# Another order of the first eight seven-product steps at each feed-forward start

## The chip, the cores and the metric

One core of a Trainium2 chip runs the whole program. The metric is the device time of one execution in microseconds (us); lower is better. Three runs of the kernel before gave 3456.26, 3458.66 and 3461.72 us, so its median is 3458.66 us.

## The reference

Two small networks run one after the other on one sequence of 512 rows of width 1024. The first has two layers of feed-forward, mixer, feed-forward; the second has two layers of mixer, feed-forward. Six feed-forward blocks in all, each

```python
def swiglu(h, w1, w3, w2):
    return (jax.nn.silu(h @ w1) * (h @ w3)) @ w2
```

with `w1` and `w3` of 1024 x 2816 and `w2` of 2816 x 1024, in float32 (in the second network these are the gate, up and down matrices). In the first network a layer's shifts, scales and gates are vectors that come from `silu(c) @ ada_w[l] + ada_b[l]`. The mixers (attention, spatial gating and a state-space scan; a gated delta rule and a short convolution) and the norms between the blocks are not touched by the change.

## The kernel before

A float32 product is made on TensorE (PE) from two rounded parts of each operand, a high and a low one: `mm3` (L102 to L107) issues high x high (L105), high x low (L106) and low x high (L107). A weight block is split by `split` (L87 to L93): ScalarE (ACT) casts it into `whi` (L90), VectorE (DVE) subtracts and writes `wlo` (L91). The hidden 2816 columns are 22 tiles of 128, the f-tiles. `ffn` (L502) does the first two of them as plain products of 512 columns (the bank `p`), then `pair_products` (L411 to L495) does the other 20 as ten pairs, i = 1 to 10. For a pair it splits the 1024-deep product into 2 x 2 blocks and makes seven block products of the kind of Strassen and Winograd in place of eight, for `w1` (w = 0) and `w3` (w = 1). One of the seven, called (i, m) here with m from 0 to 6, is 24 matmuls of 128 x 256: 2 weights x 4 chunks x 3.

- The right operands, `rhs[m]`, are quarters of the input or sums of quarters. `half_sums` (L363 to L388) makes these at each start on DVE (`bq`, and the splits into `ta` and `t`).
- The left operands come from `left` (L390 to L409). For m = 0, 1 and 4 they are raw blocks of the weights as loaded; for m = 5, 2, 3 and 6 DVE first makes a sum `sw` (L397), and (i, 2) needs the sum of (i, 5), (i, 6) that of (i, 2).
- `prepare(k + 3)` (L428 to L440) makes the split of a product three places ahead of its use in the list `seq`; the pool for `whi` and `wlo` has three buffers. `load` (L420) brings raw halves of 512 KB with SyncE's (SP's) queue (L264). The pool of raw halves has four buffers, and `nrx` more: one in the four feed-forward blocks of the first network, two in those of the second (L1758, L1863).
- In PSUM, (i, 0) opens a bank `a` and (i, 5) a bank `h`. When (i, 0) is done, ACT copies `a` to one of two banks `chain` (L478), the one of number i mod 2, and the products 2, 3 and 4 are added on there. When (i, 2) is done, ACT copies `chain` to SBUF as `sq` (L481), when (i, 3) is done once more (L487); the next product into that bank has to wait for such a copy. (i, 1) is added on to `a`, which ACT and DVE then read (L456, L457); (i, 6) is added on to `h`.
- While the first network's feed-forward blocks run, `tick` (called once per product) lets `ada_all` (L165 on) do a step of the ada vectors: a load of 512 KB (`adaraw`, L159) and one DVE instruction (L173, L175).

The order in which the products are asked for is the list `seq` (L424 to L426). A scheduler then puts the instructions on each engine in an order that it picks by its own costs, and each engine runs its own in that order. So the order on PE, ACT, DVE and SP follows from `seq`, from the buffers and from that scheduler; it is fixed when the program is built.

The starts of the six feed-forward blocks, counted from the first matmul of (1, 0), are at 65.40, 744.51, 1108.34, 1782.84, 2465.68 and 3128.11 us of the profiled execution; they are called start 1 to start 6 below.

Of the kernel before, what the change touches and what calls it, by code (L numbers as in the profile page):

```python
# [48 lines left out]
class Net:  # L49
# [361 lines left out]
    def pair_products(self, w1, w3, rhs, pool, g32, tick):  # L411


        nc = self.nc
        n = NF // 2
        raws, sts, slots = {}, {}, {}
        loads = [(i, w, k) for i in range(1, n) for k in range(2) for w in range(2)]
        ring = itertools.count()

        def load(upto):  # L420
            while loads and loads[0][0] <= upto:
                i, w, k = loads.pop(0)
                raws[i, w, k] = self.raw_half((w1, w3)[w], i * 256, k, pool if next(ring) % (4 + self.nrx) >= 4 else None)
        seq = [(1, 0)]  # L424
        for i in range(1, n):
            seq += [(i, 5), (i, 2), (i, 1), (i, 3)] + [(i + 1, 0)] * (i + 1 < n) + [(i, 4), (i, 6)]  # L426

        def prepare(k):  # L428
            if k >= len(seq):
                return  # L430
            i, m = seq[k]
            load(i)
            hi = self.wsp.tile([128, 2, 4, 128], F32R, tag="hi", name="whi")
            lo = self.wsp.tile([128, 2, 4, 128], F32R, tag="lo", name="wlo")
            for w in range(2):
                x = self.left([raws[i, w, 0], raws[i, w, 1]] if m else [raws[i, w, 0]], m, sts.setdefault((i, w), {}), pool)
                self.split(hi[:, w], lo[:, w], x)
            slots[k] = hi, lo
            if m == 5:
                load(i + 1)  # L440
        L, R = slice(0, 256), slice(256, 512)
        chain = [self.abank("chain") for _ in range(2)]
        for c in chain:

            nc.tensor.matmul(c, self.onesr, rhs[2][0].rearrange("p k n -> p (k n)")[:, 0:512], start=True, stop=True)
        for k in range(3):
            prepare(k)
            yield
        a, h, u, gs = {}, {}, {}, {}
        gtile = lambda: pool.tile([128, T], F32, tag="g", name="g", bufs=NF)  # L450
        utile = lambda: pool.tile([128, 512], F32, tag="sq", name="sq", bufs=4)

        def gated(o, x):

            s = pool.tile([128, 256], F32, tag="si", name="si", bufs=2)
            nc.scalar.activation(s, x[:, L], AF.Silu)  # L456
            nc.vector.tensor_tensor(o, s, x[:, R], op=ALU.mult)  # L457

        def gated_add(o, x, y):

            nc.vector.tensor_tensor(y, x, y, op=ALU.add)
            nc.scalar.activation(y[:, L], y[:, L], AF.Silu)  # L462
            nc.gpsimd.tensor_tensor(o, y[:, L], y[:, R], op=ALU.mult)  # L463
        for k, (i, m) in enumerate(seq):
            if m == 0:
                a[i] = self.gbank("a")
            if m == 5:
                h[i] = self.gbank("h")
            b = chain[i % 2]
            bank = {0: a, 1: a, 5: h, 6: h}.get(m, {i: b})[i]  # L470
            hi, lo = slots.pop(k)
            for w in range(2):
                for kc in range(4):
                    first = m in (0, 5) and w == 0 and kc == 0
                    self.mm3(bank[:, 256 * w:256 * w + 256], hi[:, w, kc], lo[:, w, kc], rhs[m][0][:, kc], rhs[m][1][:, kc], first, w == 1 and kc == 3,
                             skip=m not in (0, 5))
            if m == 0:
                nc.scalar.copy(b, bank)  # L478
            elif m == 2:
                u[i, 2] = utile()  # L480
                nc.scalar.copy(u[i, 2], b)  # L481
            elif m == 1:
                gs[i] = [gtile(), gtile()]
                gated(gs[i][0][:, L], a.pop(i))
            elif m == 3:
                u[i, 3] = utile()
                nc.scalar.copy(u[i, 3], b)  # L487
                gated_add(gs[i][1][:, R], h[i], u.pop((i, 3)))
            elif m == 4:
                gated(gs[i][1][:, L], b)  # L490
            elif m == 6:
                gated_add(gs[i][0][:, R], h.pop(i), u.pop((i, 2)))
                g32 += gs.pop(i)
            prepare(k + 3)
            tick(0)  # L495
# [1424 lines left out]
```

## Time and profile before

| | |
|---|---|
| median of three runs | 3458.66 us (3456.26 to 3461.72) |
| the profiled execution | 3459.09 us, its span 3457.4 us |
| PE busy | 3341.9 us, 97% of the span |
| DVE, ACT, POOL busy | 73%, 46%, 11% |
| granted TensorE clock, mean over the span | 0.989 |

PE is TensorE's matmuls, PEld its weight loads. A row of the timeline gives the start, the length, the engine, the line and the operation of an instruction, then in brackets how long its engine was idle before it and what ended that. Matmuls are pipelined: a row of 0.28 us is followed by the next after about 0.12 us where nothing is waited for. A row of a view by stretches gives the busy time of each engine between two times, the granted clock as a share of full speed, and what the DMA engines did.

### The profile page before, as it was taken

To read this page: it belongs to the slowest core of one execution; us is meant where nothing else is said; L and a number is where in the kernel's file an instruction comes from. 1 tells how busy PE (TensorE), PEld (TensorE's weight loads), DVE (VectorE), ACT (ScalarE), POOL (GpSimd) and SP (SyncE) were. 2 spreads that over 40 slices of the span, in tenths; PEclk is the share of its full clock that TensorE was granted. 3 is DMA by queue.
4 is the path that set the end of the run, shared out by engine and by line. 5 is a ranking of instruction groups with operands and counts; after the bars stand their busy time and mean duration, and the time that the engine had idled before them with its cause. 6 is when DMAs were issued, how large, how long until landed. Compare 5 with 4: busy or idle time off the path is not lost.

```text
span 3457.4 us, 56915 instructions
## 1 busy us (share of the span) xinstructions
PE 3341.9 (97%) x22138; PEld 2893.9 (84%) x22138; DVE 2530.1 (73%) x4666; ACT 1597.5 (46%) x3331; POOL 372.1 (11%) x427
## 2 busy tenths in 40 slices
PE   7999999999999999989999998999999999999999
PEld 6998776689988998866689987778999877789987
DVE  7997677789877997777789846765786357559753
ACT  3553336545533553336645533534555345345542
POOL 0221000002200210000001101101121001011200
PEclk9999999999999999999999999999999999999999
DMA  7558251335563557251334442213333321233332
GB/s 248 177 172 268 85 153 50 99 104 159 161 211 109 165 162 253 86 154 50 98 104 135 128 135 82 62 51 121 110 98 123 120 70 45 62 130 108 123 108 75
DMA packets 316270, 428.51 MB, mean 124 GB/s; under 512 B 24222, under 2 KB 255168, under 8 KB 316000
## 3 DMA queue, kind: packets, MB, share of 16 engines
q1 hardware_dynamic: 309884, 423.22, 38.3%
q8 instruction: 174, 2.85, 0.3%
q10 hardware_dynamic: 6116, 1.65, 0.2%
q14 instruction: 96, 0.79, 0.1%
HBM read 401.22 MB, written 23.59 MB: 123 GB/s over the span
## 4 chain that ended last, share of the span: by engine, by line
PE 83%; DVE 8%; ACT 3%; DMA 2%; issue 2%; POOL 1%; SPq 0%; DVEq 0%; POOLq 0%; ACTq 0%
PE acc L106 8%; PE acc L107 8%; PE acc L105 8%; PE chain L105 5%; PE chain L107 5%; PE chain L106 5%; PE g L105 4%; PE g L106 3%; PE g L107 3%; PE h L107 3%; PE h L105 3%; PE h L106 3%; PE a L107 3%; PE a L105 3%; PE a L106 3%
## 5 line engine op out<-in xcount | busy, mean ns | idle before, releaser
L91 DVE TENSOR_TENSOR wlo<-raw,whi 128x512 fp32r<-128x512 f32 (+1 forms) x700 | 534.6, 784 | 344.2 <-ACT whi L90 336.5
L90 ACT CAST whi<-raw 128x512 fp32r<-128x512 f32 (+1 forms) x700 | 473.9, 696 | 627.7 <-PE acc L107 234.4
L106 PE MATMUL acc<-wlo,ghi 128*128 128x512 f32 x992 | 393.1, 396 | 0.0
L90 ACT CAST whi<-sw 128x512 fp32r<-128x512 f32 x480 | 291.2, 618 | 219.2 <-PE chain L106 100.4
L107 PE MATMUL acc<-whi,glo 128*128 128x512 f32 x992 | 391.5, 395 | 0.0
L105 PE MATMUL acc<-whi,ghi 128*128 128x512 f32 x992 | 391.1, 394 | 0.0
L463 POOL TENSOR_TENSOR g<-sq 128x256 f32<-128x256 f32 x120 | 242.7, 2022 | 1163.1 <-ACT sq L462 1073.3
L91 DVE TENSOR_TENSOR wlo<-sw,whi 128x512 fp32r<-128x512 f32 x480 | 322.8, 689 | 46.8 <-ACT whi L90 46.6
L107 PE MATMUL a<-hThi,wlo 128*128 128x256 f32 x960 | 270.3, 282 | 11.6 <-DVE wlo L91 11.6
L105 PE MATMUL chain<-t,whi 128*128 128x256 f32 x960 | 269.8, 281 | 8.1 <-ACT sq L487 8.1
L105 PE MATMUL g<-hThi,whi 128*128 128x512 f32 x576 | 239.5, 416 | 32.0 <-DVE oT L895 23.2
L105 PE MATMUL a<-hThi,whi 128*128 128x256 f32 x960 | 269.9, 281 | 0.0
L106 PE MATMUL a<-hTlo,whi 128*128 128x256 f32 x960 | 269.4, 281 | 0.0
L107 PE MATMUL chain<-t,wlo 128*128 128x256 f32 x960 | 269.1, 280 | 0.0
L106 PE MATMUL chain<-t,whi 128*128 128x256 f32 x960 | 269.0, 280 | 0.0
L106 PE MATMUL g<-hTlo,whi 128*128 128x512 f32 x576 | 236.2, 410 | 0.0
L107 PE MATMUL g<-hThi,wlo 128*128 128x512 f32 x576 | 235.5, 409 | 0.0
L105 PEld LDWEIGHTS acc<-whi,ghi 128*128 128x128 f32 x992 | 186.3, 188 | 46.1 <-issue 0.3
L106 PEld LDWEIGHTS acc<-wlo,ghi 128*128 128x128 f32 x992 | 186.3, 188 | 44.3
L107 PEld LDWEIGHTS acc<-whi,glo 128*128 128x128 f32 x992 | 186.2, 188 | 43.7
L397 DVE TENSOR_TENSOR sw<-raw 128x512 f32<-128x512 f32 x240 | 165.1, 705 | 52.2 <-DMA raw<-in_ffn_w_gate_dram 23.3
L107 PEld LDWEIGHTS a<-hThi,wlo 128*128 128x128 f32 x960 | 181.2, 189 | 13.0 <-DVE wlo L91 13.0
(480 smaller groups left out, 8756.9 us busy)
## 6 DMA issues: line engine op xcount, KB each, us to landing
raw<-in_ffn_w_dram SPq DMA_DIRECT2D x264, 512.0 KB, 4.3
adaraw<-in_ada_w_dram SPq DMA_DIRECT2D x128, 512.0 KB, 4.7
raw<-in_w_in_dram SPq DMA_DIRECT2D x136, 256.0 KB, 3.6
raw<-in_ffn_w_gate_dram SPq DMA_DIRECT2D x44, 512.0 KB, 4.0
raw<-in_ffn_w_up_dram SPq DMA_DIRECT2D x44, 512.0 KB, 4.9
raw<-in_ffn_w_down_dram SPq DMA_DIRECT2D x44, 512.0 KB, 3.3
xdram<-x SPq DMA_DIRECT2D x36, 512.0 KB, 2.6
x<-xdram SPq DMA_DIRECT2D x36, 512.0 KB, 7.0
```

What stands on the lines that cost most here:

```text
L90: self.last_copy = self.nc.scalar.copy(hi, src)
L91: self.last_rest = (eng or self.nc.vector).tensor_tensor(lo, src, hi.bitcast(F32), op=ALU.subtract)
L105: mm(out, w_hi, m_hi, start=start, stop=False, skip_group_check=skip)
L106: mm(out, w_hi, m_lo, start=False, stop=False, skip_group_check=skip)
L107: mm(out, w_lo, m_hi, start=False, stop=stop, skip_group_check=skip)
L397: nc.vector.tensor_tensor(o, x, y, op=op)
L463: nc.gpsimd.tensor_tensor(o, y[:, L], y[:, R], op=ALU.mult)
```

## The change

The list `seq` gets other first entries; from the pair i = 2 on it is as it was.

```diff
-        seq = [(1, 0)]
-        for i in range(1, n):
+
+        seq = [(1, 0), (1, 1), (2, 0), (1, 5), (1, 2), (1, 3), (1, 4), (1, 6)]
+        for i in range(2, n):
             seq += [(i, 5), (i, 2), (i, 1), (i, 3)] + [(i + 1, 0)] * (i + 1 < n) + [(i, 4), (i, 6)]
```

Before, the list began (1, 0), (1, 5), (1, 2), (1, 1), (1, 3), (2, 0), (1, 4), (1, 6), (2, 5). Now it begins (1, 0), (1, 1), (2, 0), (1, 5), (1, 2), (1, 3), (1, 4), (1, 6), (2, 5). No instruction is added or taken away on any engine; outside of the six starts each engine's order is the same. All lines behind the list move by one (the copy of L478 stands at L479 in the changed kernel, and so on).

On PE at start 2, the end of the product in front of (1, 3) and the beginning of (1, 3) before; `chain_7730` is the bank for i = 1, `whi_7832` belongs to (1, 1) and `whi_7863` to (1, 3):

```order
L107 MATMUL a_7806<-hThi_7272,wlo_7833 128x256
L105 MATMUL a_7806<-hThi_7272,whi_7832 128x256
L106 MATMUL a_7806<-hTlo_7273,whi_7832 128x256
L107 MATMUL a_7806<-hThi_7272,wlo_7833 128x256
L105 MATMUL chain_7730<-t3_7683,whi_7863 128x256
L106 MATMUL chain_7730<-t3_7684,whi_7863 128x256
L107 MATMUL chain_7730<-t3_7683,wlo_7864 128x256
```

and in the changed kernel, where `whi_7863` belongs to (1, 2) and `whi_7905` to (1, 3):

```order
L107 MATMUL chain_7730<-ta_7682,wlo_7864 128x256
L105 MATMUL chain_7730<-ta_7682,whi_7863 128x256
L106 MATMUL chain_7730<-ta_7682,whi_7863 128x256
L107 MATMUL chain_7730<-ta_7682,wlo_7864 128x256
L105 MATMUL chain_7730<-t3_7683,whi_7905 128x256
L106 MATMUL chain_7730<-t3_7684,whi_7905 128x256
L107 MATMUL chain_7730<-t3_7683,wlo_7906 128x256
```

(1, 3) now follows (1, 2) directly in the same bank, and (1, 4) follows (1, 3) there; what stood between them, (1, 1) and (2, 0), is moved ahead. Only half of (2, 0) goes as far as the list says: its second half (`w3`) stands on PE inside (1, 3) at starts 1 to 4, because the raw half that it needs is loaded into a buffer that is read until the sums of (1, 3) are made. At starts 5 and 6, with one buffer more, all of (2, 0) stands ahead of (1, 5).

On ACT at start 2, around the two copies of `chain_7730`, before (`whi_7905` is of (2, 0), `whi_7940` of (1, 4), `whi_7975` of (1, 6)):

```order
L90 CAST whi_7863<-sw_7869 128x512
L481 COPY sq_7903<-chain_7730 128x512
L90 CAST whi_7905<-raw_7788 128x512
L90 CAST whi_7940<-raw_7737 128x512
L456 ACTIVATE si_7937<-a_7806 128x256
L90 CAST whi_7940<-raw_7739 128x512
L90 CAST whi_7975<-sw_7977 128x512
L487 COPY sq_7970<-chain_7730 128x512
L90 CAST whi_7975<-sw_7981 128x512
```

and now (`whi_7940` is of (1, 4), `whi_7792` of (2, 0), `whi_7972` of (1, 6)):

```order
L90 CAST whi_7940<-raw_7737 128x512
L90 CAST whi_7940<-raw_7739 128x512
L482 COPY sq_7970<-chain_7730 128x512
L90 CAST whi_7792<-raw_7786 128x512
L90 CAST whi_7972<-sw_7974 128x512
L479 COPY chain_7729<-a_7879 128x512
L90 CAST whi_7972<-sw_7978 128x512
L488 COPY sq_8006<-chain_7730 128x512
```

The two casts of (1, 4), which stood behind the first copy, now stand in front of it; a cast of (1, 6), the copy of `a` for i = 2 and a second cast of (1, 6) stand in front of the second copy, where one cast stood. At start 4 the second cast of (2, 0) stands in front of the first copy too, at start 1 between the two casts of (1, 4).

On ACT at start 5, where `whi_25868` is of (1, 4), `whi_25900` of (1, 6) and `whi_25939` of (2, 5):

```order
L90 CAST whi_25868<-raw_25671 128x512
L90 CAST whi_25868<-raw_25673 128x512
L90 CAST whi_25900<-sw_25902 128x512
L482 COPY sq_25898<-chain_25664 128x512
L90 CAST whi_25900<-sw_25906 128x512
L90 CAST whi_25939<-sw_25941 128x512
L488 COPY sq_25934<-chain_25664 128x512
L90 CAST whi_25939<-sw_25945 128x512
```

Here one cast stands in front of each of the two copies.

## Rows read from the trace of the kernel before

**Rows 1.** The page: busy time and share of the span; the chain by engine.
```profile
PE 3341.9 (97%) x22138; PEld 2893.9 (84%) x22138; DVE 2530.1 (73%) x4666; ACT 1597.5 (46%) x3331; POOL 372.1 (11%) x427
...
PE 83%; DVE 8%; ACT 3%; DMA 2%; issue 2%; POOL 1%; SPq 0%; DVEq 0%; POOLq 0%; ACTq 0%
```

**Rows 2.** Stretches: (1, 0) to (2, 5); columns: PE, PEld, DVE, ACT, POOL, PEclk, DMA share, GB/s.
```profile
65.40:95.21 29.81, 27.22 (x198) 26.07 (x196) 25.69 (x43) 14.14 (x30) 1.08 (x1) 0.89 0.42 124
744.51:776.61 32.10, 27.41 (x193) 26.48 (x192) 29.16 (x48) 15.63 (x29) 1.27 (x1) 0.84 0.31 99
1108.34:1139.19 30.85, 26.17 (x193) 25.26 (x192) 29.10 (x48) 15.76 (x29) 1.27 (x1) 0.89 0.32 103
1782.84:1814.38 31.54, 26.66 (x193) 25.75 (x192) 29.19 (x49) 15.64 (x29) 1.26 (x1) 0.89 0.32 101
2465.68:2488.21 22.53, 22.53 (x194) 22.53 (x193) 22.28 (x38) 13.03 (x25) 4.88 (x1) 1.00 0.45 138
3128.11:3150.64 22.53, 22.53 (x194) 22.52 (x192) 22.35 (x38) 13.04 (x25) 4.88 (x1) 1.00 0.46 133
```

**Rows 3.** Stretches at half clock, at starts 1 to 4.
```profile
70.60:77.40 6.80, 6.15 (x27) 5.88 (x28) 6.80 (x12) 3.29 (x6) 0.00 (x0) 0.50 0.26 63
749.90:760.10 10.20, 8.82 (x38) 8.30 (x39) 8.72 (x16) 4.42 (x8) 0.00 (x0) 0.50 0.19 51
1115.10:1121.90 6.80, 5.45 (x25) 5.04 (x24) 6.80 (x12) 3.80 (x7) 0.00 (x0) 0.50 0.11 25
1790.90:1797.70 6.80, 6.45 (x28) 6.16 (x29) 6.04 (x11) 3.44 (x7) 0.00 (x0) 0.50 0.26 75
```

**Rows 4.** Timeline of PE at start 2, the end of (1, 0) and the first of (1, 5).
```profile
745.88 0.38 PE L107 MATMUL a<-hThi,wlo 128*128 128x256 f32 x1 [0.97 <-DVE wlo L91]
...
750.09 0.58 PE L107 MATMUL a<-hThi,wlo 128*128 128x256 f32 x1 [2.52 <-DVE wlo L91]
...
753.78 0.58 PE L105 MATMUL h<-ta,whi 128*128 128x256 f32 x1 [1.19 <-ACT whi L90]
```

**Rows 5.** Timelines of PE at starts 1, 3 and 4, the first of (1, 5).
```profile
71.25 0.58 PE L105 MATMUL h<-ta,whi 128*128 128x256 f32 x1 [1.37 <-ACT whi L90]
...
1116.41 0.58 PE L105 MATMUL h<-ta,whi 128*128 128x256 f32 x1 [1.19 <-ACT whi L90]
...
1791.08 0.58 PE L105 MATMUL h<-ta,whi 128*128 128x256 f32 x1 [1.19 <-ACT whi L90]
```

**Rows 6.** Timeline of PE at start 5, the first of (1, 0) and of (1, 5).
```profile
2465.68 0.28 PE L105 MATMUL a<-hThi,whi 128*128 128x256 f32 x1
...
2468.49 0.28 PE L105 MATMUL h<-ta,whi 128*128 128x256 f32 x1
```

**Rows 7.** Timeline of ACT at start 2: the copy of `a`, two casts.
```profile
752.63 0.57 ACT L478 COPY chain<-a 128x512 f32<-128x512 f32 x1 [3.14 <-PE a L107]
...
756.27 0.61 ACT L90 CAST whi<-raw 128x512 fp32r<-128x512 f32 x1
756.79 0.61 ACT L90 CAST whi<-sw 128x512 fp32r<-128x512 f32 x1
```

**Rows 8.** Waits of PE on a copy: line waited for, us in total, times, longest.
```profile
PE chain L105 <- ACT sq L487: 8.1, 6, 1.5
```

**Rows 9.** Timelines of ACT and PE at two block ends, (10, 3) before (10, 4).
```profile
270.11 1.04 ACT L90 CAST whi<-raw 128x1024 fp32r<-128x1024 f32 x1 [1.39 <-PE chain L106]
271.06 0.58 ACT L487 COPY sq<-chain 128x512 f32<-128x512 f32 x1
...
271.69 0.39 PE L105 MATMUL chain<-t,whi 128*128 128x256 f32 x1 [1.50 <-ACT sq L487]
...
949.25 0.38 PE L105 MATMUL chain<-t,whi 128*128 128x256 f32 x1 [0.63 <-ACT sq L487]
```

**Rows 10.** DMA issues of the page: KB each, median us from issue to landing.
```profile
raw<-in_ffn_w_dram SPq DMA_DIRECT2D x264, 512.0 KB, 4.3
```

**Rows 11.** Timeline of DVE at start 1: a sum behind transposes of small vectors.
```profile
82.68 0.69 DVE L397 TENSOR_TENSOR sw<-raw 128x512 f32<-128x512 f32 x1 [3.34 <-PE colps L136]
```

**Rows 12.** A stretch around the 1.50 us wait of 271.69.
```profile
265.00:280.00 15.00, 13.50 (x103) 12.80 (x103) 11.26 (x18) 8.67 (x15) 5.13 (x2) 1.00 0.92 329
```

## The prediction

> **What bounds the kernel now.** I read the page first. PE is busy for 97% of the span and makes 83% of the chain that ended last [rows 1]: DVE at 73% and ACT at 46% do not bound the program as a whole, so time is to be had only where PE stands still or runs slowly. Then I took the six places that the change touches, as stretches from the first matmul of (1, 0) to the first of (2, 5), eight products each [rows 2]. Starts 5 and 6 take 22.53 us, PE is busy in all of it and the clock is full: nothing can be gained there. Starts 1 to 4 take 29.81, 32.10, 30.85 and 31.54 us, so they lose 7.3, 9.6, 8.3 and 9.0 us against 22.53, 34.2 us together, 1.0% of the program. In these four DVE is busy for 26 to 29 us. It makes the sums of `half_sums` there while PE already multiplies, and is late.
>
> What the loss is made of, two views show. One is the granted clock: 0.50 (1.2 of 2.4 GHz) in stretches of 6.8, 10.2, 6.8 and 6.8 us [rows 3]. Half of the 30.6 us is up to 15.3 us lost. The other is PE's timeline. At start 2 PE waits 0.97 and 2.52 us for `wlo` inside (1, 0), then 1.19 us for the first `whi` of (1, 5) [rows 4]; at starts 1, 3 and 4 that last wait is 1.37, 1.19 and 1.19 us [rows 5]. The waits in front of (1, 5) make 4.94 us. These are the waits that the change reaches: the casts of (1, 5) wait for two `sw` sums, which stand behind the half sums on DVE. The waits inside (1, 0) come before anything that is moved, and stay.
>
> A product at full clock takes 2.81 us (2465.68 to 2468.49 [rows 6]), at half clock twice that.
>
> **The change part by part.** Nothing is added or removed, so the price lies in waits and in the clock.
>
> (a) (1, 1) in place of (1, 5) behind (1, 0), starts 1 to 4. Its left operand is raw, so its cast needs no DVE sum and is done early; the 1.37 + 3 x 1.19 us go. What is late next is the copy of `a`: (1, 1) adds on to the bank that ACT must first copy to `chain`, and that copy cannot start before (1, 0) ends. The copy takes 0.57 us [rows 7], and where PE waited for a copy with nothing in front of it the wait was 0.63 us [rows 9]. Two matmuls of (2, 0) stand between and cover 0.24 us at full clock, 0.4 at half; I take 0.4 at start 1 and 0.25 at the others. That is -0.95 at each of starts 1 to 4, -3.8 in all. At starts 5 and 6 six matmuls of (2, 0), 0.7 us, cover the copy: 0.
>
> (b) (1, 3) directly behind (1, 2). Before, (1, 1) lay between and hid the copy to `sq` (L481). Now PE must wait for it. ACT takes its instructions in order, and in front of the copy stand the casts of (1, 4), whose buffer comes free only when (1, 2) ends. The nearest rows are the waits on L487: six, 8.1 us in all [rows 8]. At 271.69 a cast of 1.04 us stood in front of the copy and PE waited 1.50 us; at 949.25 PE had other work first and waited 0.63 [rows 9]. The other four then make 8.1 - 1.50 - 0.63 = 6.0, 1.5 each. Two casts of 128x512, 0.52 us apart [rows 7], are the same 1.04 us. So starts 2 and 3 pay 1.5 each. Starts 5 and 6 have one cast in front: 0.52 + 0.58 = 1.1 each. Bounds: 0.63 if the casts are done by then, 2.2 if three stand in front.
>
> (c) (1, 4) directly behind (1, 3), with the copy L487 exposed. At starts 2 and 3 the second half of (2, 0) has to end before ACT can do a cast of (1, 6); then come the copy of `a`, another cast and the copy wanted: 0.52 + 0.58 + 0.52 + 0.58 = 2.2 us, less 0.24 us for the two matmuls of (1, 3) that PE has left: 1.95 each. At starts 5 and 6 again one cast and one copy: 1.0 each. Same bounds.
>
> (d) The second half of (2, 0) needs a raw half whose load is issued when DVE has made the first sum of (1, 3), and which lands 4.3 us later [rows 10]. At starts 2 and 3 ACT casts it behind the copy of (b), and PE has ten matmuls of (1, 3) first: covered, 0, or 1 us if DVE is later than that. At start 4 the cast stands in front of that copy, so the copy waits for the load. Laid out from where (1, 0) ends, DVE's order reaches that sum some 3 us before (1, 2) ends (my estimate), so the load lands 1.3 us after that end, then 0.52 + 0.58: 2.4 in place of 1.5; and (c) is 0.5 there, since (2, 0) ends earlier inside (1, 3): 2.9 for (b) to (d). At start 1 an ada load stands in SP's queue ahead of it, DVE's sums wait 3.34 us behind transposes (L136) [rows 11], and the cast of (2, 0) stands between the two of (1, 4). I take 0.85 for (b), 0.9 for (c), 1.45 for the load and 1.5 for sums that come late behind the transposes, all four estimates: 4.7 between bounds of 1.3 (two bare waits of 0.63) and 6.3 (two of 1.5 and the 3.34 of rows 11 in full, which PE does not feel before). The ada steps that move among the products cost nothing of their own: on DVE they stand behind sums and splits that PE needs sooner.
>
> (e) The clock. At starts 1 and 4 it falls at 70.6 and 1790.9 [rows 3], late in the wait in front of (1, 5) (69.88 to 71.25 and 1789.89 to 1791.08 [rows 5]) that (a) shortens. If it stays up, half of 6.8, 3.4 us, is saved; I count that in full at these two. At start 3 it falls at 1115.1, just before that wait begins (1115.22), so the waits inside (1, 0) may be what brings it down: half of 3.4, 1.7. At start 2 it falls at 749.9, in the wait of 2.52 us that stays [rows 4]; there only the longer stay, 10.2 against 6.8 us, can go: 1.7. At start 1 the new waits of (d) can bring a fall of their own, 3.4 us with one chance in four: +0.85. Together -3.4 - 1.7 - 1.7 - 3.4 + 0.85 = -9.35. Bounds: -15.3, and above nothing if the new waits keep the clock down as long or longer.
>
> The sum by starts: start 1, -0.95 - 3.4 + 0.85 + 4.7 = +1.2; start 2, -0.95 - 1.7 + 1.5 + 1.95 = +0.8; start 3 the same, +0.8; start 4, -0.95 - 3.4 + 2.9 = -1.45; starts 5 and 6, 1.1 + 1.0 = +2.1 each. That is **+5.6 us**. PE goes on without a break behind each start, so nothing takes it up later. On the profiled 3459.09 it gives 3464.7; that execution lies 0.4 us above the median of three, so I say 3465.
>
> A rule of the Trainium skill speaks against such an order. "Perfetto Trace Analysis", section Optimizing Tensor Performance, Matmuls, says that independent groups of matmuls should rotate through PSUM banks, so that the emptying of one bank overlaps the next group. By it alone each of the 18 places where a product now follows into the bank being copied would show one copy, 18 x 0.58 = 10.4 us, and the sum would be 10.4 - 4.94 - 9.35 = -3.9, some 3455. The trace agrees on the direction but not on the size: casts queued in front make it 1.50 [rows 9], other matmuls in between make it less.
>
> **The rivals.** *A, the copies come bare and the clock stays up: faster.* With the casts done before the products end, (b) and (c) cost 0.63 each, 12 x 0.63 = 7.6; (a) gives -3.8 and the clock all 15.3: 3459.1 + 7.6 - 3.8 - 15.3 = 3447.6. For it: two of the four falls lie in the wait that goes. Against it: the casts of (1, 4) wait for a buffer that (1, 2) holds, and the fall at start 2 lies before the change. With the clock up but the waits as priced it is 3464.7 - 5.95 = 3459, no change.
>
> *B, the clock falls in the new waits: slower.* Place: PE between (1, 2) and (1, 4) at starts 1 to 4, where two waits of 1.5 to 2 us lie within 5 us, right behind the waits inside (1, 0). If the clock gains nothing it is 3464.7 + 9.35 = 3474; with a further stretch of 6.8 us at starts 2 and 3, 3481. It decides from one more half-rate stretch of 3.4 us on. Against it: a 1.50 us wait at a block end left the clock at 1.00 [rows 12]. For it: waits of 2.52 and 1.19 us in a row did bring it down. By the Trainium skill ("TensorE: Matmul & The Clock Gate", section A second HAM failure mode: psum-queue depth-cycling) short idle times between groups that cycle through PSUM make the clock go up and down, which would be this rival and some 3474; rows 12 do not bear that out.
>
> *C, the change hardly does what it says: no change.* (2, 0) already slips back half way, and if PE finds its waits filled by the other bank the whole comes to 3459, within 2 us.
>
> **How the numbers follow.** A measurement here can tell some 0.2%, 6.9 us, from no change. The forecast (3460 to 3470) has 0.50, of it 0.30 within 0.2% and 0.20 above, since its middle lies near that edge. A has 0.12 faster, and 0.10 with the waits as priced, no change. B has 0.20, slower. C has 0.08. So faster 0.12, within 0.48, slower 0.40. The range 3453 to 3478 leaves out A's faster part (0.12) and the upper end of B (some 0.06), and takes in the bounds of start 1.
>
> **What would show it.** In the changed profile PE should wait for L479 before (1, 1), 0.2 to 0.5 us, and the waits for `whi` before (1, 5) should be gone at starts 1 to 4; PE's waits for a copy to `sq` should grow from 8.1 us by 15 or more, in twelve new places; starts 5 and 6 should take 24.6 in place of 22.53 us at full clock; of the stretches at 0.50 that of start 2 should remain, and those of starts 1 and 4 be gone. I am wrong if starts 5 and 6 stay at 22.5 (the price of (b) and (c)), or if the number and length of the half-clock stretches come out otherwise (the price of (e)).

## The result, and the profile after

The changed kernel takes 3479.05 us (median of six runs, 3473.20 to 3491.71); the kernel before takes 3456.77 us in the same comparisons (3453.77 to 3461.72, six runs). The ratio is 1.0064, its 95% interval 1.0052 to 1.0077: 22 us slower, 18 to 27. The prediction said 3465, and 3453 to 3478.

The profiled execution took 3483.53 us, its span is 3481.8, 24.4 us more than before. The page's line of busy times and its chain by engine, to be held against [rows 1]:

```profile
PE 3349.8 (96%) x22138; PEld 2897.4 (83%) x22138; DVE 2535.9 (73%) x4666; ACT 1598.1 (46%) x3331; POOL 342.3 (10%) x427
...
PE 81%; DVE 9%; DMA 3%; ACT 3%; issue 2%; POOL 1%; SPq 0%; DVEq 0%; ACTq 0%; POOLq 0%
```

PE is busy 7.9 us longer, though it runs the same matmuls; the other 16.5 us are added idle time. Where, the stretches show. In the changed kernel two matmuls of (2, 5) stand inside (1, 4), so both kernels are cut here from the first matmul of (1, 0) to the first of (2, 2), nine products. The columns are as in [rows 2]. Before:

```profile
65.40:98.02 32.62, 30.03 (x221) 28.88 (x220) 28.50 (x47) 16.69 (x35) 1.08 (x1) 0.90 0.41 121
744.51:779.42 34.91, 30.22 (x217) 29.29 (x216) 31.97 (x53) 17.20 (x32) 1.62 (x2) 0.85 0.31 94
1108.34:1142.04 33.70, 29.02 (x217) 28.11 (x216) 31.95 (x51) 17.32 (x32) 1.79 (x2) 0.90 0.31 97
1782.84:1817.23 34.39, 29.51 (x217) 28.60 (x216) 32.04 (x53) 17.20 (x32) 1.78 (x2) 0.90 0.31 98
2465.68:2491.02 25.34, 25.34 (x217) 25.34 (x216) 25.09 (x43) 14.60 (x28) 5.00 (x2) 1.00 0.40 125
3128.11:3153.46 25.35, 25.35 (x218) 25.34 (x216) 24.25 (x41) 14.18 (x27) 4.88 (x1) 1.00 0.43 126
```

and the changed kernel:

```profile
65.29:98.95 33.66, 28.39 (x221) 26.62 (x220) 32.46 (x54) 16.35 (x33) 1.39 (x2) 1.00 0.48 152
746.76:785.14 38.38, 29.98 (x217) 28.67 (x216) 33.97 (x54) 16.21 (x30) 2.24 (x2) 0.91 0.37 113
1116.39:1151.63 35.24, 28.12 (x217) 27.03 (x216) 33.52 (x54) 16.23 (x30) 2.12 (x2) 0.95 0.38 122
1793.28:1828.12 34.84, 28.95 (x218) 27.54 (x217) 33.08 (x54) 16.20 (x30) 2.10 (x2) 0.95 0.37 120
2479.60:2507.85 28.25, 26.45 (x218) 25.72 (x216) 26.86 (x46) 13.73 (x26) 1.39 (x2) 1.00 0.35 112
3147.75:3176.01 28.26, 26.46 (x218) 25.73 (x217) 26.67 (x45) 13.68 (x26) 0.74 (x1) 1.00 0.36 113
```

The first column after the times is the length: +1.04, +3.47, +1.54, +0.45, +2.91, +2.91 us, 12.3 together. The granted clock (third from the right) is higher at starts 1 to 4, and PE is busy for less time there, and still every start is longer. So these stretches hold half of the 24.4 us. PE's timeline at start 2 shows the waits inside one, and a wait ahead of it:

```profile
743.62 0.73 PE L446 MATMUL chain<-ta,onesr 128*128 128x512 f32 x2 [1.67 <-ACT ta L90]
...
747.95 0.39 PE L107 MATMUL a<-hThi,wlo 128*128 128x256 f32 x1 [0.79 <-DVE wlo L91]
...
752.17 0.39 PE L107 MATMUL a<-hThi,wlo 128*128 128x256 f32 x1 [2.52 <-DVE wlo L91]
...
754.98 0.58 PE L105 MATMUL a<-hThi,whi 128*128 128x256 f32 x1 [0.23 <-ACT chain L479]
...
767.12 0.36 PE L105 MATMUL chain<-t,whi 128*128 128x256 f32 x1 [1.70 <-issue]
...
769.85 0.58 PE L105 MATMUL a<-hThi,whi 128*128 128x256 f32 x1 [1.30 <-ACT whi L90]
...
776.49 0.39 PE L105 MATMUL chain<-t,whi 128*128 128x256 f32 x1 [1.87 <-ACT sq L488]
```

The wait of 1.19 us before (1, 5) [rows 4] is gone; 0.23 before (1, 1) stands in its place, and the two waits inside (1, 0) are much as before. New are 1.70 before (1, 3), 1.30 before the second half of (2, 0), 1.87 before (1, 4), and 1.67 before L446, the small matmul that opens the two `chain` banks. ACT's timeline names what PE waits for at 767.12, where PE's row says only "issue":

```profile
765.40 1.14 ACT L90 CAST whi<-raw 128x512 fp32r<-128x512 f32 x2 [0.54 <-PE chain L106]
766.45 0.58 ACT L482 COPY sq<-chain 128x512 f32<-128x512 f32 x1
769.18 0.62 ACT L90 CAST whi<-raw 128x512 fp32r<-128x512 f32 x1 [2.15 <-DMA raw<-in_ffn_w_dram]
774.31 0.62 ACT L90 CAST whi<-sw 128x512 fp32r<-128x512 f32 x1 [4.51 <-PE a L106]
774.83 0.58 ACT L479 COPY chain<-a 128x512 f32<-128x512 f32 x1
775.35 0.61 ACT L90 CAST whi<-sw 128x512 fp32r<-128x512 f32 x1
775.86 0.58 ACT L488 COPY sq<-chain 128x512 f32<-128x512 f32 x1
```

Two casts, then the copy: this is the queue that the prediction laid out for (1, 3), and the last four rows are the one for (1, 4). The third row is the cast of (2, 0), late by its load.

The wait of L446 was not foreseen. ACT's rows ahead of it, then DVE's:

```profile
739.79 0.61 ACT L90 CAST t<-bq 128x512 fp32r<-128x512 f32 x1
742.43 0.62 ACT L90 CAST whi<-raw 128x512 fp32r<-128x512 f32 x1 [2.02 <-DMA raw<-in_ffn_w_dram]
742.95 0.61 ACT L90 CAST ta<-bq 128x512 fp32r<-128x512 f32 x1
```

```profile
741.24 0.68 DVE L380 TENSOR_TENSOR bq<-bq 128x512 f32<-128x512 f32 x1
743.60 0.69 DVE L91 TENSOR_TENSOR ta<-bq,ta 128x512 fp32r<-128x512 f32 x1 [1.67 <-ACT ta L90]
```

The cast at 742.43 is the first of (1, 1). It stands on ACT between two casts of the half sums, and its raw half has not landed. ACT waits 2.02 us for it, the half sums' cast `ta` behind it waits too, DVE stands still for 1.67 us in the stage where DVE is the one that is late, and PE waits for `ta`. At starts 3 and 4 L446 waits 1.13 and 0.89 us: 3.7 us that lie ahead of the stretches above.

At start 5, where nothing is late, PE's rows show what a wait costs besides its idle time:

```profile
2493.78 0.28 PE L107 MATMUL chain<-ta,wlo 128*128 128x256 f32 x1
2495.23 0.36 PE L105 MATMUL chain<-t,whi 128*128 128x256 f32 x1 [1.17 <-issue]
2495.43 0.28 PE L106 MATMUL chain<-t,whi 128*128 128x256 f32 x1
2495.55 0.28 PE L107 MATMUL chain<-t,wlo 128*128 128x256 f32 x1
...
2498.04 0.28 PE L107 MATMUL chain<-t,wlo 128*128 128x256 f32 x1
2498.95 0.39 PE L105 MATMUL h<-ta,whi 128*128 128x256 f32 x1 [0.63 <-ACT whi L90]
2499.18 0.28 PE L106 MATMUL h<-ta,whi 128*128 128x256 f32 x1
2499.43 0.39 PE L105 MATMUL chain<-t,whi 128*128 128x256 f32 x1
```

The matmul behind 2493.78 was due 0.12 us later, at 2493.90, and began at 2495.23: 1.33 us lost where the row lists 1.17, since the idle time is counted from the end of the matmul before, 0.28 us after its start. The first steps after it are 0.20 to 0.25 us instead of 0.12. The two waits list 1.80 us and the stretch is 2.91 us longer.

Of the 24.4 us, 12.3 are in the stretches and 3.7 in the waits of L446. Two more pieces lie where no instruction was moved. Behind starts 5 and 6 the products keep a slower pace, 845 matmuls in 100 us where there were 855. Before and after, behind start 5:

```profile
2520.00:2620.00 100.00, 100.00 (x855) 100.00 (x854) 79.87 (x133) 55.04 (x108) 24.48 (x10) 1.00 0.36 118
```

```profile
2520.00:2620.00 100.00, 100.00 (x845) 100.00 (x845) 80.39 (x130) 54.60 (x106) 14.88 (x10) 1.00 0.33 106
```

The experiments come back to it. It makes 1.9 us for each of the two blocks. And the second network's first mixer, up to start 5, takes 476.9 us against 472.6; one load of `w_out` is awaited longer there, before:

```profile
2390.24 0.62 ACT L90 CAST wx<-raw 128x512 fp32r<-128x512 f32 x1 [1.50 <-DMA raw<-in_w_out_dram]
```

and in the changed kernel:

```profile
2401.40 0.62 ACT L90 CAST wx<-raw 128x512 fp32r<-128x512 f32 x1 [3.34 <-DMA raw<-in_w_out_dram]
```

12.3 + 3.7 + 3.8 + 4.3 = 24.1. That this comes so close to 24.4 is in part chance: the four blocks in front have other paces too, which take back 0.8 us together, and about 1 us is not placed.

### The profile page after: what moved, and what is told of

It reads as the page before. It is cut to its first block, busy times and chain, and to the rows that moved or that the text cites. A ratio compares the mean times of both kernels' runs of the same rounds, so it can differ in the third digit from the quotient of the medians.

```text
span 3481.8 us, 56923 instructions
## 1 busy us (share of the span) xinstructions
PE 3349.8 (96%) x22138; PEld 2897.4 (83%) x22138; DVE 2535.9 (73%) x4666; ACT 1598.1 (46%) x3331; POOL 342.3 (10%) x427
## 4 chain that ended last, share of the span: by engine, by line
PE 81%; DVE 9%; DMA 3%; ACT 3%; issue 2%; POOL 1%; SPq 0%; DVEq 0%; ACTq 0%; POOLq 0%
PE acc L107 8%; PE acc L106 8%; PE acc L105 8%; PE chain L105 4%; PE chain L106 4%; PE chain L107 4%; PE g L105 3%; PE g L106 3%; PE g L107 3%; PE a L105 3%; PE a L107 3%; PE a L106 3%; PE h L105 3%; PE h L107 3%; PE h L106 3%
## 5 line engine op out<-in xcount | busy, mean ns | idle before, releaser
L464 POOL TENSOR_TENSOR g<-sq 128x256 f32<-128x256 f32 x120 | 214.7, 1789 | 1206.1 <-ACT sq L463 1206.1
L105 PE MATMUL g<-hThi,whi 128*128 128x512 f32 x576 | 239.9, 416 | 30.6 <-DVE oT L896 22.1
L105 PEld LDWEIGHTS chain<-t,whi 128*128 128x128 f32 x960 | 182.0, 190 | 21.7 <-ACT sq L488 14.3
```

What stands on the lines that cost most here:

```text
L105: mm(out, w_hi, m_hi, start=start, stop=False, skip_group_check=skip)
```

## The experiments

**The two ends of the program by themselves.** The list is chosen by `nrx`, which is 2 in the last two feed-forward blocks and 1 in the first four:

```diff
-        seq = [(1, 0)]
-        for i in range(1, n):
+        seq = NEW if self.nrx == 2 else OLD
+        for i in range(2, n):
```

(`NEW` and `OLD` are the first eight entries after and before; the second kernel has `nrx == 1`.)

> The new order at starts 5 and 6 alone, the old one at starts 1 to 4. The trace of the changed kernel shows two waits of PE for a copy there, 1.17 and 0.63 us idle, which set PE back by 2.9 us in all, and after them a product takes 2.85 us to the end of the block where it took 2.815 before, 1.9 us more per block. Theory (exposed copies, and a slower pace of PE that a wait leaves behind): 2 x 2.9 + 2 x 1.9 = +9.6 us, 3466, with products of 2.85 us behind both starts. Rival (exposed copies alone; the slower pace was an accident of that run): +5.8 us, 3463, products of 2.815. The prediction on record: +4.2 us, 3461.

Measured: 3466.10 us, ratio 1.0028 (1.0017 to 1.0039), 6 to 13 us slower. In its trace both starts wait 1.17 and 0.63 us idle and take 28.39 us, 3.05 more each, and the pace behind both is the fast one. So the theory is right on the copies and wrong on the pace: the waits do not leave it behind. Its 3466 was met by luck, then, since 3.8 us of its sum were that pace: the stretches hold 6.1 of the 9.7 us that the ratio says, and the rest is not placed.

> The new order at starts 1 to 4 alone. If the two halves of the change add up, this is the change's +22 less what the order at starts 5 and 6 costs: +12 us (3469) where that is 9.6, +16 (3473) where it is 5.8. Starts 5 and 6 should take 22.5 us again, with products of 2.815 us behind them, if the slower pace comes from the waits there. The prediction on record: +1.4 us, 3458.

Measured: 3470.98 us, ratio 1.0036 (1.0023 to 1.0048), 8 to 17 us slower. The two parts add up to the whole, 9.7 + 12.4 = 22.1. Behind starts 5 and 6, in the old order and without a wait, the pace is the slow one in this run:

```profile
2520.00:2620.00 100.00, 100.00 (x845) 100.00 (x845) 81.13 (x134) 54.36 (x107) 19.69 (x10) 1.00 0.33 106
3180.00:3280.00 100.00, 100.00 (x845) 100.00 (x844) 80.34 (x132) 54.19 (x106) 22.22 (x11) 1.00 0.36 118
```

That settles it against the waits as the pace's cause.

**The cast that waits for its load.** The splits of (1, 1) and (2, 0) are queued on ACT behind the last cast of the half sums:

```diff
+        self.last_half = self.last_copy
...
-                self.split(hi[:, w], lo[:, w], x)
+                if k in (1, 2):
+                    with self.tc.issue_after(self.last_half.ins):
+                        self.split(hi[:, w], lo[:, w], x)
+                else:
+                    self.split(hi[:, w], lo[:, w], x)
```

> The whole change, but the casts of (1, 1) and (2, 0) are put on ACT behind the last cast of the half sums. In the changed kernel a cast of (1, 1) stands between those, waits for its load (2.02 us at start 2), and the small matmul of L446 that opens the chain banks waits for the half sums behind it: 1.67, 1.13 and 0.89 us at starts 2 to 4. Theory (these waits are a loss of their own): they go, and with them 5 us of the 22, to 3474. Rival (DVE is the limit there, and the waits inside (1, 0) grow by what is saved): 3479, unchanged, with waits of more than 2.5 us inside (1, 0).

Measured: 3472.82 us, ratio 1.0044 (1.0032 to 1.0057), 6 to 7 us less than the change, although the two intervals overlap a little. All three waits of L446 are gone, and the waits inside (1, 0) at start 2 are 0.96 and 2.54 us, as before. The theory holds: this queue was a loss of its own, by these medians a quarter to a third of the whole.

**An order with the copies covered.** At starts 1 to 4 `seq` begins (1, 0), (1, 1), (1, 5), (1, 2), (2, 0), (1, 3), (1, 4), (1, 6), with the casts of (1, 1) and (1, 5) behind the half sums; starts 5 and 6 have the old order.

> At starts 1 to 4 the order (1, 0), (1, 1), (1, 5), (1, 2), (2, 0), (1, 3), (1, 4), (1, 6) with the casts of (1, 1) and (1, 5) behind the half sums on ACT; at starts 5 and 6 the old order. (2, 0) lies in part between (1, 2) and (1, 3) and inside (1, 3), so both copies are covered; only the copy of a before (1, 1) is not (0.63 idle). Theory (the exposed copies, not the two products without a sum, make the change slow): the wait of 1.2 to 1.4 us before (1, 5) goes at four starts for 0.6, -2.5 us, and of the half clock 30.6 us some 15 stay, -7: 3447. Rival (DVE's half sums set the end of these starts, whatever the order): the waits come back before (1, 5) or (1, 2), 3457. Rival (the clock falls as before): 3454.

Measured: 3465.86 us, ratio 1.0019 (1.0010 to 1.0028), 3 to 10 us slower than before: none of the three expectations. At start 2 the copies are covered (at starts 1 and 4 PE still waits 0.50 and 0.92 us for the second one), and 0.66 us before (1, 1) came as expected. But the second half of (2, 0) is now wanted before its raw half can land:

```profile
769.39 0.39 PE L105 MATMUL a<-hThi,whi 128*128 128x256 f32 x1 [2.85 <-ACT whi L90]
```

At starts 1, 3 and 4 this wait is 1.15, 0.67 and 0.95 us. The wait moved from the copy to the load, a rival that I had not named, and 23.8 of 30.6 us of half clock stayed.

**Both kernels once more, for their traces.** An empty line is added to each.

> The kernel before once more, with an empty line added, for its trace. In the runs so far a product in the long stretches behind the starts takes 2.815 or 2.85 us, one or the other for a whole block: 2.815 behind starts 5 and 6 before and in the run with the new order at these two alone, 2.85 in the other four, also where the order there is the old one. If the pace belongs to the program, it is 2.815 behind both again and the pieces behind starts 1 to 4 are at the same paces as before. If it belongs to the run, at least one of these differs, by up to 2.3 us per block. The half clock at starts 1 to 4: 30.6 us again if it belongs to the program.

> The changed kernel once more, with an empty line added, for its trace. If the paces belong to the program: 2.85 us per product behind starts 5 and 6 again. The stretches from (1, 0) to (2, 2) should repeat in any case, as their waits do: 33.7, 38.4, 35.2, 34.8, 28.2, 28.2 us, within what the half clock moves (1.7 us per 3.4 us of it), and the three waits of L446, 1.67, 1.13 and 0.89 us.

Measured, one run each: 3456.24 and 3474.58 us, 18.3 apart. The stretches repeat to 2.2 us, and most of what differs goes with the half clock and with the load at start 2 (0.67 us of wait instead of 1.30): 32.62, 34.06, 33.53, 34.10, 25.34, 25.34 us with 27.2 us of half clock for the kernel before, 35.21, 36.16, 35.26, 33.40, 28.15, 28.25 with 10.2 for the changed one, 11.4 us more (12.3 in the first pair). L446 waits 1.15, 1.28 and 0.61 us. The paces do not repeat: the changed kernel now runs 855 matmuls in 100 us behind start 5 and 845 behind start 6, and the kernel before has other paces behind starts 1 to 4 than in its first trace. So the pace belongs to the run, and one trace can be some 4 us off by it.

**The half sums on another engine.** The order is the old one; the three instructions that make `t4`, for each half, go to POOL:

```diff
-            b22, b21 = b(1, 1, nc.vector), b(1, 0, nc.vector)
+            b22, b21 = b(1, 1, nc.vector), b(1, 0, nc.gpsimd)
...
-            sub(b21, b21, b22)
+            nc.gpsimd.tensor_tensor(b21, b21, b22, op=ALU.subtract)
...
+                if nm == "t4":
+                    nc.scalar.copy(t[nm][0][:, sl], x)
+                    nc.gpsimd.tensor_tensor(t[nm][1][:, sl], x, t[nm][0][:, sl].bitcast(F32), op=ALU.subtract)
+                else:
+                    self.split(t[nm][0][:, sl], t[nm][1][:, sl], x)
```

> The old order; of the 24 DVE instructions of the half sums the six that make t4 (needed by (1, 4) only) go to POOL, which is idle there. Theory (DVE's half sums set the waits inside (1, 0) and before (1, 5), so the lever is DVE's work, not the order of the products): up to 6 x 0.60 = 3.6 us of the 4.7 us of waits go at each of starts 1 to 4, and with them much of the half clock's 15 us: 3456.8 - 4 x 3 - 8 = 3437. Rival (POOL is slow, 4 us for such an instruction and more beside DVE, and (1, 4) waits for t4): 3457 or more, with PE waiting for POOL before (1, 4). The prediction on record says nothing on this.

Measured: 3478.35 us, ratio 1.0061 (1.0048 to 1.0074), as slow as the change. The rival was right on POOL and wrong on the place; the wait is inside (1, 0), 5.29 us at start 2. POOL's row, ACT's and DVE's say why:

```profile
739.29 5.22 POOL L384 TENSOR_TENSOR bq<-bq 128x512 f32<-128x512 f32 x1 [5.51 <-DVE bq L380]
```

```profile
744.54 0.62 ACT L387 CAST t<-bq 128x512 fp32r<-128x512 f32 x1 [4.75 <-POOL bq L384]
745.07 0.61 ACT L90 CAST ta<-bq 128x512 fp32r<-128x512 f32 x1
```

```profile
745.71 1.35 DVE L91 TENSOR_TENSOR ta<-bq,ta 128x512 fp32r<-128x512 f32 x1 [2.36 <-ACT ta L90]
746.98 1.74 DVE L380 TENSOR_TENSOR bq<-bq 128x512 f32<-128x512 f32 x1
```

While DVE works without a break the subtraction on POOL takes 5.22 us. Behind DVE's pause, from 745 on, POOL's instructions take 1.3 to 1.7 us, and it is DVE's instruction of 0.68 us that takes 1.35 to 1.75 where one of them overlaps it. And ACT again holds a cast of the half sums behind one that waits, 4.75 us. The Trainium skill has the rule on the two engines ("SBUF — State Buffer", section Who interferes with whom): a DVE instruction with two inputs in SBUF contends with a GpSimd instruction that reads SBUF. This run agrees. Whether less work on DVE would shorten these starts is left open by it.

**The copies ahead of the casts.** On top of the kernel with the casts of the half sums first, the splits of (1, 4) are asked for after the copy of (1, 2), those of (1, 6) and (2, 5) after the copy of (1, 3):

```diff
-            prepare(k + 3)
+            if k in (4, 5):
+                with self.tc.issue_after(copied.ins):
+                    for q in {4: (6,), 5: (7, 8)}[k]:
+                        prepare(q)
+            elif k != 3:
+                prepare(k + 3)
```

(`copied` is the copy to `sq` just issued.) The scheduler gave DVE another order at starts 1 to 4 as well: at start 2, for one, two steps of the ada vectors fall between (1, 0) and (2, 2) instead of three.

> The whole change with the casts of (1, 1) and (2, 0) behind the half sums as before, and besides the casts of (1, 4) put behind the copy of (1, 2) to sq, those of (1, 6) and (2, 5) behind the copy of (1, 3). Theory (a wait for a copy is as long as the casts in front of it make it): 1.7 and 1.87 us idle at starts 2 and 3 and 1.17 at 5 and 6 become 0.63, some 8 us less than the 3472.8 measured with the casts of the half sums alone: 3465. Rival (the casts held back come late themselves, and PE waits for whi or wlo of (1, 4) and (1, 6) in their place): 3473 or more.

Measured: 3455.76 us, ratio 0.9989 (0.9980 to 0.9998), faster than expected, and not slower than before any more. On ACT at start 2 both copies now come right behind the product that they wait for, with no cast in front:

```profile
759.58 0.58 ACT L487 COPY sq<-chain 128x512 f32<-128x512 f32 x1 [0.61 <-PE chain L107]
...
764.99 0.59 ACT L493 COPY sq<-chain 128x512 f32<-128x512 f32 x1 [1.31 <-PE chain L107]
```

PE's waits there are:

```profile
760.27 0.36 PE L105 MATMUL chain<-t,whi 128*128 128x256 f32 x1 [0.72 <-issue]
...
763.73 0.39 PE L105 MATMUL a<-hThi,whi 128*128 128x256 f32 x1 [1.11 <-ACT whi L90]
```

and none before (1, 4); at starts 5 and 6 they are 0.78 and 0.67. The six stretches are 8.0 us shorter than with the casts in front (186.2 against 194.2), just what was expected. But by the medians the two runs differ by 17 us and by the ratios by 19, 12 at the least; so by these figures more than half of what this edit gave lies outside of these stretches, and no trace shows where (the two executions that were traced differ by 6.9 us only).

**The same at either end alone.**

> The new order with the copies ahead of the casts at starts 1 to 4, the old order at starts 5 and 6. In the run with it at all six, (1, 0) to (2, 2) took 131.1 us at starts 1 to 4 against 135.6 and 134.3 in the two traces of the kernel before, with 6.8 us of half clock against 30.6 and 27.2, and 27.55 us at starts 5 and 6 against 25.34. Theory (two products without a sum gain at the four starts where DVE is behind, through the clock; the bare copies cost 2.2 us at each of the other two): 3 to 4.5 us faster than before by the stretches, some 3453 where the kernel before gives 3457. Rival (what the run with all six gained was an accident of its paces): within 2 us of before.

Measured: 3451.81 us, ratio 0.9984 (0.9976 to 0.9993), 2 to 8 us faster than the kernel before. This version beats both kernels. Its starts 1 to 4 take 31.38, 33.36, 31.11 and 32.58 us, 128.4 against 135.6 and 134.3, with 3.4 us of half clock. Three other traces with the old order there (the new order at starts 5 and 6 alone, with and without the copies first, and the control below) give 133.0 to 133.7, so 5 to 7 us are gained.

> The new order with the copies ahead of the casts at starts 5 and 6 alone. No clock, no late half sums there: what is left is the price of two bare waits for a copy, 0.78 and 0.67 us idle. Theory: +2.2 us at each by the stretch from (1, 0) to (2, 2) (27.55 against 25.34), +4.4 in all, 3461 where the kernel before gives 3457, and less than the 9.3 us that the same order cost there with casts in front of the copies. Rival (a wait leaves a slower pace behind it, whatever its length): +8 us or more, and products of 2.85 us behind both starts.

Measured: 3460.38 us, ratio 1.0007 (0.9998 to 1.0016), +2.4 us. The stretches are 27.52 us, 2.2 more each. The 4.4 us lie inside the interval (-0.7 to 5.5); the rival's 8 do not, and the pace behind both starts is the fast one. With casts in front the same order cost 9.7 us, now 2.4. The stretches show only 1.7 of these 7 us (28.39 against 27.52, twice); the rest is open here too. This version also holds the casts of (1, 1) and (2, 0) behind the half sums, as the first did not.

**A control.** One more small matmul of L445 at each of starts 1 to 4, in the old order:

```diff
-        for c in chain:
+        for c in chain + chain[:1] * (self.nrx == 1):
```

> A control: the old order everywhere, and one more small matmul of L445 into a chain bank at each of starts 1 to 4 (which PE does while it waits, 0.23 us each, 1 us in all). In the second network's first mixer, whose order of instructions no run changed, the stretch from the end of the fourth block's products to start 5 took 472.0 to 472.8 us in four traces whose program is the old one up to there, and 474.2 to 476.9 in eight traces whose program differs ahead of it, with a wait for a load of w_out of 1.4 to 1.6 us in the four and of 2.5 to 3.6 in the eight. If any difference ahead brings this, it is 474 or more here too, and the time 3 to 5 us over the kernel before. If it comes from the products' new order, 472.5 and +1 us, 3458 where the kernel before gives 3457.

Measured: 3457.87 us, ratio 1.0003 (0.9994 to 1.0012); one of the twelve executions took 13472.89 us, for no known cause, and is not in the ratio. The mixer takes 470.8 us, so it is not true that any difference ahead lengthens it, although the wait for `w_out` is 2.22 us, between the two groups. What makes it 2 to 4 us longer in every kernel with a changed start ahead of it is open.

## Why the prediction was wrong

The sum by starts was +1.2, +0.8, +0.8, -1.45, +2.1, +2.1, and came out as +1.04, +3.47, +1.54, +0.45, +2.91, +2.91 in the stretches.

- **Step (a)** is where it failed. That (1, 1) would wait only for the copy of `a` was right: 0.23 us at start 2, 0.25 expected. But the step said of (1, 1) that "its cast needs no DVE sum and is done early", and stopped there. A cast that is early in ACT's order and whose data is late holds up all that stands behind it, here the casts of the half sums. The prediction used ACT's order for the copies and not for this cast, which stands there between two casts of the half sums; it put this wait at nothing. Cost: 3.7 us listed at L446, some 6 by the run that takes the cast away from there.
- **Steps (b) and (c)** had the right mechanism, place and idle time: 1.70 and 1.87 us at start 2 for 1.5 and 1.95, 1.17 at start 5 for 1.1. For (c) at starts 5 and 6 the row lists 0.63 for 1.0, because PE waits for the cast of (2, 5) and does two matmuls of it while the copy runs. The sign named beforehand, 15 us or more on waits for a copy to `sq` in twelve new places, did not come: the rows list 10.0 us more, in seven, since at starts 1, 4, 5 and 6 a late cast of (2, 0) or (2, 5) is what PE waits for in some of them. What was mis-sized is their worth, +2.1 us for a start that lost 2.9 to 3.05. A listed idle time leaves out the 0.16 us by which matmuls overlap and the slow first steps. With 27 waits in the six stretches where there were 13, the overlap alone is 2.2 us. The prediction took the idle column for the loss. The runs with the copies first show that most of the loss goes when the copies come first: with casts in front 3472.8, behind 3455.8. That it went by way of these waits is shown for 8.0 of the 17 us; for the rest, DVE's new order in that run is a rival that was not tested alone.
- **Step (d)** took 0 for the load at start 2 and it was 1.30 (0.67 in the second trace); at start 3, 0 was right. At start 1 the waits behind (1, 5) list 3.2 us (4.7 expected), at start 4 they list 2.2 (2.9 expected).
- **Step (e)** was nearly right in size: 13.6 us of half clock instead of 30.6 save 8.5 us, 9.35 expected. The places were other: none at start 1, two of 3.4 us at start 2, one at start 3, and at start 4 one in the new waits, so that start 4 saved 1.7 where 3.4 was counted.
- **Rival B**, slower by the clock with 3474 to 3481, gave nearly the time that was measured and is not what happened: the clock fell for less time, not more. By the Trainium skill ("TensorE: Matmul & The Clock Gate", section A second HAM failure mode: psum-queue depth-cycling), which tells of a kernel whose short idle times between groups made the clock fall and rise again and again, the new short waits should have brought it down; here the stretches with the most waits had the higher clock.
- **Rival A** was wrong for the change, since the casts stood in front. But its conditions are those of the version that won, where the copies come nearly bare and the clock stays up. The rule on rotating banks ("Perfetto Trace Analysis", section Optimizing Tensor Performance, Matmuls, in the Trainium skill) gives, as an estimate with this trace's copy of 0.58 us, one bare copy for each of the four places at starts 5 and 6, 2.3 us; the run with bare copies there alone measured +2.4, and its trace 4.4.

The prediction's sum has no term for the rest of the 24.4 us of the trace: 3 to 4 us were the pace of that run, and 4.3 (2.5 in the second pair of traces) the longer mixer, which the experiments tie to the changed starts and not to a cause. That cause stays open.

## What to carry to other kernels

Before an instruction is moved ahead on an engine that works in order, ask when its data lands, and who stands behind it there: the loss shows up on other engines. When a copy becomes the thing that PE waits for, look at what is queued in front of the copy: putting it first took most of the loss away here, though the traces place only a part of that in the waits for it. Take the loss from a wait as the step from one start of a matmul to the next, less the usual one, and not as the idle time listed.

## What was not expected of the hardware

PE mostly keeps one of two paces over a long stretch at full granted clock, 117.3 or 118.7 ns per matmul of 128x256 (855 or 845 in 100 us). The pace differs from block to block and, for the same program, from run to run; in the block behind start 4 of the run with the copies first it went from 117.3 to 118.7 where two products came slower. In the run of the best version the two last blocks, both in the old order and without a wait, have one each:

```profile
2520.00:2620.00 100.00, 100.00 (x855) 100.00 (x854) 82.11 (x134) 55.22 (x108) 20.86 (x10) 1.00 0.33 106
3180.00:3280.00 100.00, 100.00 (x845) 100.00 (x844) 80.01 (x131) 54.48 (x106) 17.75 (x10) 1.00 0.34 111
```

In some blocks it was 120.0 ns, all through the one behind start 4 of the same run. A block of ten pairs is 2 us longer at the slower pace, so differences of a few us between two single traces are not to be explained before the paces are compared.
